# Squares, gating, value products and row transposes moved to other engines and steps in a hybrid retention and attention layer

## The chip, the cores and the metric

The kernel runs on one core of one Trainium2 chip. The metric is the device time of one execution in microseconds; the median of several runs counts. A core has TensorE (PE, with its weight loads PEld), VectorE (DVE), ScalarE (ACT), GpSimd (POOL) and SyncE (SP), which issues nearly all transfers of this kernel. Each engine works through its own instructions in the order in which the program gives them.

## The reference

One layer of a diffusion transformer over 2048 rows of width 1024, with 256 rows of context. It has a bidirectional retention (4 heads, in chunks of 128 rows), a grouped-query attention (8 query heads, 2 key heads, 64 wide, over context and rows) and a squared-relu MLP:

```python
h = _modulate(_rmsnorm(x, norm1_g), sh1, sc1)
rq, rk, rv, rg, aq, ak, av = jnp.split(h @ w_in, SPLIT_IDX, axis=-1)
...
ret, _, _ = _bidir_retention(rq_h, rk_h, _heads(rv, RET_HEADS), log_gamma, s_f, s_b)
ret = _ret_out(ret, rg, ret_gn_g)
...
att = _latent_attention(q, k, v, kc, vc)
x = x + g1 * (jnp.concatenate([ret, att], axis=-1) @ w_out)
h2 = _modulate(_rmsnorm(x, norm2_g), sh2, sc2)
x = x + g2 * (jnp.square(jax.nn.relu(h2 @ w_ff1)) @ w_ff2)
...
return _rmsnorm(x, final_norm_g)
```

## The kernel before

All products keep nearly full precision: each operand is split into a high and a low half, and three matmuls (high by high, high by low, low by high) stand for one. The order of work is written out by hand. Each part of the program enters its functions in a table by step and phase, and a loop runs the steps one after another and the phases of a step in a fixed order. So the order on every engine is the order of this table, and an engine runs ahead of the others only as far as waits and buffers let it.

**Projections** (to about 650 us). `do(s, part, fn)` enters a function; a step `s` is the product of one tile of 128 rows with one block of 512 columns of w_in (L1063 to L1065). The parts of a step run in the order hi, evac, turned, low, vec, pool, root, aux, turn, load, store. Beside the products run the tables of decay for the retention (`decay_tables`: a logarithm as a series on VectorE, `power` on VectorE, exponentials on ScalarE), the first 12 forward states of the retention (`forward_state`: load k and v of a chunk, weigh k by the decay on GpSimd at L1027, four products on TensorE at L1032, update on VectorE, store; one state in three steps), and the values' halves (`value_parts`). The tile `early` holds the tables' working space first and then k, v and the state. Keys are turned on TensorE (L744) and copied from PSUM by VectorE (L749). The low halves of the weights are made on VectorE (L516).

**Attention** (about 650 to 1650 us). Steps are entered with `on(k, phase, fn)`; the phases run in this order:

```python
PHASES = ("begin", "scores", "piece", "maximum", "early", "exp", "cast", "low", "chain", "pe", "values")
PHASES += ("late", "dma")
```

32 groups (16 tiles of rows by 2 key heads) of 18 steps each follow one another. In a step, TensorE makes one tile of scores (L209, L210) of one group and one piece (L172) for the row maxima of the next group; VectorE reduces the piece (L185), ScalarE takes the exponential (L215) into `p32` (three buffers of two steps each). Every two steps ScalarE casts a pair of tiles to fp16 (`phi`, L219), the low half `plo` is made on GpSimd (L226, five pairs of nine) or on VectorE (L228, in two parts), and TensorE multiplies both halves with the values (L242, L243).

Among these steps lie the retention (`retention(k0)`: five forward and two backward states at steps from `k0`, then one chunk in every RF = 35 steps), the gated halves of w_out (`output_weights`) and the output product of one tile of rows in every 35 steps (`output_tile`). That function turns the retention's and the attention's rows (L1588), multiplies, adds the input on VectorE (L1610), scales the new rows on GpSimd (`norm`, L1630), transposes them (`transpose_x`, L1635), applies the modulation on VectorE (L1640) and adds the shift on GpSimd (L1645). All transposes use PSUM bank 1, as the retention's heads do. For four of the tiles, `h_pair` then forms sums of rows for the MLP. `more_keys` fills the additional key rows `ks2` of a group.

**Up phase** (about 1650 to 2210 us) and **down phase** (to the end). The MLP is done with seven products in place of eight (Strassen's scheme): for every block of 256 of the 4096 columns, seven sums of quarters of w_ff1 are made on GpSimd and split on ScalarE (L1813) and VectorE (L1819). `up_part` multiplies them with seven sums of the rows; `up_out` combines the results on VectorE (L1849). For every finished quarter, relu on ScalarE (L1853) and a square on GpSimd (L1854) follow, and a store two steps on. In the same steps `seven` prepares w_ff2: it loads two blocks of rows, multiplies them by the gate (`gated`, L1892), makes sums on GpSimd (L1896) and splits on ScalarE (L1901) and VectorE (L1907). The phases of a step here are:

```python
FPHASES = ("pe", "sum", "hi", "lo", "relu", "out", "square", "late", "dma")
```

Of the kernel before, what the change touches and what calls it, by code (L numbers as in the profile page):

```python
# [13 lines left out]
F16 = mybir.dt.float16  # L14
BF16 = mybir.dt.bfloat16
I32 = mybir.dt.int32
AF = mybir.ActivationFunctionType
# [39 lines left out]
def layer_kernel(ctx: ExitStack, tc: tile.TileContext, a: dict, out: bass.AP):  # L57
# [89 lines left out]
    class Group:  # L147
# [69 lines left out]
        def cast(self, j):  # L217
            hi = self.hi[j] = pp.tile([P, 2, 512], F16, name="phi", tag="phi")
            nc.scalar.activation(hi, self.p[j], AF.Copy)  # L219

        def low(self, j, i=None):
            if i in (None, 0):
                self.lo[j] = pp.tile([P, 2, 512], F16, name="plo", tag="plo")
            lo, p, hi = self.lo[j], self.p[j], self.hi[j]
            if i is None:
                nc.gpsimd.tensor_tensor(lo, p, hi, op=ALU.subtract)  # L226
            else:
                nc.vector.tensor_tensor(lo[:, i], p[:, i], hi[:, i], op=ALU.subtract)  # L228
# [38 lines left out]
    with ExitStack() as st, tc.manual_schedule():  # L267
# [671 lines left out]
        def decay_tables(s):  # L939
# [14 lines left out]

            def series():
                u, w1, z, zz, lg = (x[v] for v in ("u", "w1", "z", "zz", "lg"))
                nc.vector.tensor_scalar(w1, u, -1.0, 1.0, op0=ALU.mult, op1=ALU.add)
                nc.vector.tensor_scalar(z, u, -1.0, 2.0, op0=ALU.mult, op1=ALU.add)
                nc.vector.reciprocal(z, z)
                nc.vector.tensor_mul(z, z, u)  # L960
                nc.vector.tensor_mul(zz, z, z)
                nc.vector.tensor_scalar(lg, zz, 1.0 / 17, 1.0 / 15, op0=ALU.mult, op1=ALU.add)
                for k in range(13, 0, -2):
                    nc.vector.tensor_mul(lg, lg, zz)
                    nc.vector.tensor_scalar_add(lg, lg, 1.0 / k)
                nc.vector.tensor_mul(lg, lg, z)
                nc.vector.tensor_scalar_mul(lg, lg, -2.0)

# [36 lines left out]
            do(s + 2, "hi", base)  # L1005
            do(s + 3, "aux", series)
            do(s + 4, "hi", log)
            do(s + 5, "aux", choose)
            for h in range(4):
                do(s + 6, "aux", power, h)  # L1010
                do(s + 7, "hi", tables, h)
            do(s + 7, "hi", rest)
            do(s + 8, "aux", diagonal)

        states = {}

        def forward_state(s, c):

            k, v = (early[:, 512 * i : 512 * i + 512].rearrange("p (h d) -> p h d", h=4) for i in range(2))
            st = early[:, 1536:2048].rearrange("p (h d) -> p h d", h=4)  # L1020

            def load():
                for to, src in ((k, rk_d[c]), (v, rv_d[c])):
                    nc.sync.dma_start(to.rearrange("p h d -> p (h d)"), src)

# [20 lines left out]

            do(s, "load", load)
            do(s + 1, "pool", weigh)
            do(s + 2, "turn", product)
            do(s + 3, "vec", update)  # L1050
            if c > 0:
                do(s + 4, "store", keep_state)

# [293 lines left out]
    def attention():  # L1347
        for n, g in enumerate(groups):
# [28 lines left out]
        return NK * len(groups) + LAG + 8  # L1377

# [198 lines left out]
    def output_tile(t, k, last):  # L1577
# [263 lines left out]
    def up_out(at, n, i, hf):  # L1841
# [10 lines left out]
        def done(r, f, tg):  # L1852
            on(at + 1, "relu", lambda: nc.scalar.activation(r, r, AF.Relu, scale=scu))  # L1853
            on(at + 2, "square", lambda: nc.gpsimd.tensor_tensor(r, r, r, op=ALU.mult))  # L1854
            on(at + 4, "dma", store_u, ITEMS[n][0], hf, 2 * tg + f, r)
# [23 lines left out]
    def seven(b0, source, tiles, low, kinds, scale=None, gate=None):  # L1879
# [10 lines left out]
        def gated(g):  # L1890
            w, eng = x["raw", g], nc.vector if g else nc.gpsimd
            eng.tensor_tensor(w, w, ff["g2"], op=ALU.mult)  # L1892

# [356 lines left out]
```

## Time and profile before

| | |
|---|---|
| median of three runs | 2811.19 us (2808.23 to 2811.27) |
| profiled execution | 2814.1 us |
| its span, first to last instruction | 2812.3 us |
| TensorE busy | 2673.6 us (95%) |
| VectorE busy | 2122.4 us (75%) |
| GpSimd busy | 1886.5 us (67%) |
| ScalarE busy | 1463.5 us (52%) |
| mean granted clock of TensorE | 0.990 |

A line such as `PE o L242 <- POOL plo L226: 17.9, 15, 2.5` (the whole span) reads: TensorE, before an instruction of line 242 that writes `o`, stood idle until an instruction of GpSimd at line 226 that writes `plo` was done; 17.9 us in all, in 15 waits, the longest 2.5 us. In a row of stretches, the span of the stretch comes first, then the busy time of each engine with the number of its instructions, then the granted clock of TensorE as a share of full speed, the transfers' share and GB/s. In a row of a group of instructions, busy time in us and the mean of one in ns follow the count, and then the idle time of the engine just before them and what ended it. In a row in order of time, the start and the length in us come first.

### The profile page before, as it was taken

Reading aid. Unit: us, or ns where it says so; the run is one execution under the profiler, and the core shown is the slowest. Engines: PE = TensorE matmul, PEld = TensorE weight load, DVE = VectorE, ACT = ScalarE, POOL = GpSimd, SP = SyncE. Lnnn points to the kernel's source line nnn. Section 1 sums busy time; section 2 is a strip of 40 time slices with the busy share of each in tenths; the row PEclk is TensorE's granted clock in tenths of the full one; section 3 lists DMA queues with packets and bytes.
Section 4 is the critical chain, followed back from the end, with each engine's and each line's share of the span. In section 5 each row is a group of like instructions: output and inputs, shape, how many; then the busy total and the mean of one; then the engine's idle time right before and its main releaser. Section 6 shows DMA issues by size and latency. Waiting matters only on the chain. (4 is left out here: it accounts for less than half of the span.)

```text
span 2812.3 us, 45879 instructions
## 1 busy us (share of the span) xinstructions
PE 2673.6 (95%) x16756; PEld 1605.7 (57%) x16756; DVE 2122.4 (75%) x3061; ACT 1463.5 (52%) x2442; POOL 1886.5 (67%) x1453
## 2 busy tenths in 40 slices
PE   6999999997799999999999999999999999999998
PEld 3878788875566666556666644444444444444444
DVE  3678847777987787777877568999999766556686
ACT  2534443325777777777777745544555422222243
POOL 2537427535766667886666679988888766666686
PEclk9999999999999999999999999999999999999999
DMA  6776876856211214332121174666777757575543
GB/s 214 262 263 195 289 277 205 288 190 189 66 52 52 66 59 119 96 99 85 63 91 45 64 255 143 191 211 201 230 251 239 260 183 277 177 261 196 180 159 126
DMA packets 329775, 482.86 MB, mean 172 GB/s; under 512 B 81990, under 2 KB 192838, under 8 KB 325068
## 3 DMA queue, kind: packets, MB, share of 16 engines
q1 hardware_dynamic: 329164, 479.66, 51.6%
q8 instruction: 132, 2.16, 0.3%
q14 instruction: 95, 0.78, 0.1%
q10 hardware_dynamic: 384, 0.26, 0.0%
HBM read 327.64 MB, written 152.19 MB: 171 GB/s over the span
## 5 line engine op out<-in xcount | busy, mean ns | idle before, releaser
L185 DVE TENSOR_REDUCE nm<-mp 128x1 f32<-128x512 f32 (+1 forms) x576 | 390.1, 684 | 171.0 <-PE mp L172 145.6
L226 POOL TENSOR_TENSOR plo<-p,phi 128x1024 f16<-128x1024 f32 x160 | 355.1, 2220 | 171.4 <-ACT phi L219 141.3
L215 ACT ACTIVATE p<-st 128x512 f32<-128x512 f32 x576 | 338.7, 597 | 197.7 <-PE st L210 127.5
L1839 PE MATMUL pu<-hf,w1f 128*128 128x512 f16 x896 | 339.7, 379 | 4.6 <-DVE w1f L1819 4.4
L1837 PE MATMUL pu<-hf,w1f 128*128 128x512 f16 x896 | 339.6, 379 | 1.8 <-DVE r L1849 1.8
L2063 PE MATMUL pd<-w,uf 128*128 128x512 f16 x896 | 339.6, 379 | 0.0
L2064 PE MATMUL pd<-w,uf 128*128 128x512 f16 x896 | 339.6, 379 | 0.0
L2065 PE MATMUL pd<-w,uf 128*128 128x512 f16 x896 | 339.6, 379 | 0.0
L1838 PE MATMUL pu<-hf,w1f 128*128 128x512 f16 x896 | 339.6, 379 | 0.0
L219 ACT ACTIVATE phi<-p 128x1024 f16<-128x1024 f32 x288 | 303.9, 1055 | 0.0
L2083 POOL TENSOR_TENSOR y<-y,d 128x512 f32<-128x512 f32 x128 | 210.5, 1646 | 137.8 <-ACT uf L2052 90.8
L1065 PE MATMUL pso<-whi,hlo_l 128*128 128x512 f32 (+1 forms) x768 | 290.1, 378 | 10.6 <-DVE hlo_l L492 10.5
L1063 PE MATMUL pso<-whi,hhi_l 128*128 128x512 f32 (+1 forms) x768 | 299.1, 389 | 0.0
L1064 PE MATMUL pso<-wlo,hhi_l 128*128 128x512 f32 (+1 forms) x768 | 288.0, 375 | 0.6 <-DVE wlo L516 0.6
L242 PE MATMUL o<-wv,plo 128*128 128x65 f16 x2304 | 234.8, 193 | 25.0 <-POOL plo L226 17.9
L228 DVE TENSOR_TENSOR plo<-p,phi 128x512 f16<-128x512 f32 x256 | 239.1, 934 | 19.5 <-ACT phi L219 14.2
L242 PEld LDWEIGHTS <-plo 128*128 128x128 f16 x2304 | 206.3, 98 | 69.3 <-POOL plo L226 26.0
L243 PE MATMUL o<-wv,phi 128*128 128x129 f16 x2304 | 242.6, 220 | 0.0
L209 PE MATMUL st<-qr,ks 128*128 128x512 f16 x576 | 220.3, 383 | 8.0 <-ACT p L215 7.6
L172 PE MATMUL mp<-ks,qr 128*128 128x512 f16 x512 | 197.2, 385 | 26.2 <-DVE nm L185 25.9
L210 PE MATMUL st<-qr,ks 128*128 128x512 f16 x576 | 220.7, 383 | 0.4
L243 PEld LDWEIGHTS <-phi 128*128 128x128 f16 x2304 | 205.4, 97 | 20.7
(331 smaller groups left out, 6093.4 us busy)
## 6 DMA issues: line engine op xcount, KB each, us to landing
wm<-in_w_ff SPq DMA_DIRECT2D x64, 512.0 KB, 7.1
u<-r SPq DMA_DIRECT2D x128, 256.0 KB, 4.0
ur<-u SPq DMA_DIRECT2D x128, 256.0 KB, 6.4
y<-x SPq DMA_DIRECT2D x64, 512.0 KB, 7.2
wst<-in_w_in SPq DMA_DIRECT2D x60, 512.0 KB, 6.7
wf<-w2f SPq DMA_DIRECT2D x112, 256.0 KB, 3.6
w<-wf SPq DMA_DIRECT2D x28, 1024.0 KB, 10.8
w1r<-in_w_ff SPq DMA_DIRECT2D x48, 512.0 KB, 5.1
```

Source lines behind the costliest of these rows:

```text
L185: nc.vector.tensor_reduce(dst, src, axis=AX.X, op=ALU.max, negate=True)
L215: nc.scalar.activation(self.p[kt // 2][:, kt % 2], self.s.pop(kt), AF.Exp, scale=HD**-0.5)
L219: nc.scalar.activation(hi, self.p[j], AF.Copy)
L226: nc.gpsimd.tensor_tensor(lo, p, hi, op=ALU.subtract)
L242: mm(o[:, : HD + 1], lo[:, i, c], v[:, : HD + 1], start=False, stop=False)
L243: mm(o, hi[:, i, c], v[:, :VW], start=False, stop=last)
L1837: mm(pu[hf, i], whi, hi, start=k == 0, stop=False)
L1838: mm(pu[hf, i], whi, lo, start=False, stop=False)
L1839: mm(pu[hf, i], wlo, hi, start=False, stop=k == 3)
L2063: mm(ps, u[:, 0, b], w[:, b, 0], start=b == 0, stop=False)
L2064: mm(ps, u[:, 0, b], w[:, b, 1], start=False, stop=False)
L2065: mm(ps, u[:, 1, b], w[:, b, 0], start=False, stop=b == 3)
```

## The change

Up phase: the square runs on ScalarE, in the step after its relu, instead of on GpSimd in that step, and both gating passes run on GpSimd; before, the second was on VectorE. Attention: the products with the values come one step later, with four buffers each instead of three for `phi` and `plo`; the end of a group moves by one step with them, and the loop is one step longer. The transposes of the new rows come at steps 39 and 41 of a tile instead of 27 and 28 (but for the last but one tile, which keeps 31 and 32), and all that follows on them moves along. The retention's first steps begin four steps later, the second group's extra keys 4, 3 and 2 steps later. Projections: the products of the states stand two steps behind the weighing instead of one, with k loaded one step ahead and k and v rotating through three places of `early`; the decay tables begin one step later, with the series on three steps and the powers on two; the value parts begin two steps later.

```diff
         def cast(self, j):
-            hi = self.hi[j] = pp.tile([P, 2, 512], F16, name="phi", tag="phi")
+            hi = self.hi[j] = pp.tile([P, 2, 512], F16, name="phi", tag="phi", bufs=4)
...
-                self.lo[j] = pp.tile([P, 2, 512], F16, name="plo", tag="plo")
+                self.lo[j] = pp.tile([P, 2, 512], F16, name="plo", tag="plo", bufs=4)
...
-            def series():
+            def series(i):
...
-                for k in range(13, 0, -2):
+                for k in ((13, 11), (9, 7, 5), (3, 1))[i]:
...
-            do(s + 3, "aux", series)
-            do(s + 4, "hi", log)
-            do(s + 5, "aux", choose)
+            for i in range(3):
+                do(s + 3 + i, "aux", series, i)
+            do(s + 5, "hi", log)
+            do(s + 6, "aux", choose)
             for h in range(4):
-                do(s + 6, "aux", power, h)
-                do(s + 7, "hi", tables, h)
-            do(s + 7, "hi", rest)
-            do(s + 8, "aux", diagonal)
+                do(s + 7 + h // 2, "aux", power, h)
+                do(s + 8 + h // 2, "hi", tables, h)
+            do(s + 8, "hi", rest)
+            do(s + 10, "aux", diagonal)
...
-            k, v = (early[:, 512 * i : 512 * i + 512].rearrange("p (h d) -> p h d", h=4) for i in range(2))
-            st = early[:, 1536:2048].rearrange("p (h d) -> p h d", h=4)
+            k, v, st = (
+                early[:, 512 * i : 512 * i + 512].rearrange("p (h d) -> p h d", h=4)
+                for i in (2 * c % 3, (2 * c + 1) % 3, 3)
+            )
...
-            do(s, "load", load)
+            do(s - 1 if c else s, "load", load, k, rk_d[c])
+            do(s, "load", load, v, rv_d[c])
             do(s + 1, "pool", weigh)
-            do(s + 2, "turn", product)
-            do(s + 3, "vec", update)
+            do(s + 3, "turn", product)
+            do(s + 4, "vec", update)
             if c > 0:
-                do(s + 4, "store", keep_state)
+                do(s + 5, "store", keep_state)
...
-        value_parts(first[2, C_RK] + 4)
-        decay_tables(first[1, C_AKV] + 4)
+        value_parts(first[2, C_RK] + 6)
+        decay_tables(first[1, C_AKV] + 5)
...
-                on(k + 2 * j + 6, "values", g.values, j)
-            k += NK + 5
+                on(k + 2 * j + 7, "values", g.values, j)
+            k += NK + 6
...
-        return NK * len(groups) + LAG + 8
+        return NK * len(groups) + LAG + 9
...
-            at = k + (31 if t == 1 else 27) + q
+            at = k + (31 + q if t == 1 else 39 + 2 * q)
             on(at, "pe", transpose_x, q)
...
-        on(26 + 4 * i, "late", more_keys, 1, i)
+        on(30 + 3 * i, "late", more_keys, 1, i)
     done = attention()
-    retention(24)
+    retention(28)
...
             on(at + 1, "relu", lambda: nc.scalar.activation(r, r, AF.Relu, scale=scu))
-            on(at + 2, "square", lambda: nc.gpsimd.tensor_tensor(r, r, r, op=ALU.mult))
+            on(at + 2, "relu", lambda: nc.scalar.activation(r, r, AF.Square))
             on(at + 4, "dma", store_u, ITEMS[n][0], hf, 2 * tg + f, r)
...
         def gated(g):
-            w, eng = x["raw", g], nc.vector if g else nc.gpsimd
-            eng.tensor_tensor(w, w, ff["g2"], op=ALU.mult)
+            w = x["raw", g]
+            nc.gpsimd.tensor_tensor(w, w, ff["g2"], op=ALU.mult)
...
-                on(b0 - 2 + g, "lo" if g else "sum", gated, g)
+                on(b0 - 2 + g, "sum", gated, g)
```

More of the change, by code (lines that the diff above doesn't have):

```diff
@@ L953, in base @@
                 nc.scalar.activation(x["u"], x["lr"], AF.Exp)
-            def series():
+            def series(i):
                 u, w1, z, zz, lg = (x[v] for v in ("u", "w1", "z", "zz", "lg"))
[L957 to L962, printed above, removed]
-                for k in range(13, 0, -2):
+                if i == 0:
+                    nc.vector.tensor_scalar(w1, u, -1.0, 1.0, op0=ALU.mult, op1=ALU.add)
+                    nc.vector.tensor_scalar(z, u, -1.0, 2.0, op0=ALU.mult, op1=ALU.add)
+                    nc.vector.reciprocal(z, z)
+                    nc.vector.tensor_mul(z, z, u)
+                    nc.vector.tensor_mul(zz, z, z)
+                    nc.vector.tensor_scalar(lg, zz, 1.0 / 17, 1.0 / 15, op0=ALU.mult, op1=ALU.add)
+                for k in ((13, 11), (9, 7, 5), (3, 1))[i]:
                     nc.vector.tensor_mul(lg, lg, zz)
                     nc.vector.tensor_scalar_add(lg, lg, 1.0 / k)
-                nc.vector.tensor_mul(lg, lg, z)
-                nc.vector.tensor_scalar_mul(lg, lg, -2.0)
+                if i == 2:
+                    nc.vector.tensor_mul(lg, lg, z)
+                    nc.vector.tensor_scalar_mul(lg, lg, -2.0)
             def log():
@@ L1005, in decay_tables, with load @@
             do(s + 2, "hi", base)
-            do(s + 3, "aux", series)
-            do(s + 4, "hi", log)
-            do(s + 5, "aux", choose)
+            for i in range(3):
+                do(s + 3 + i, "aux", series, i)
+            do(s + 5, "hi", log)
+            do(s + 6, "aux", choose)
             for h in range(4):
-                do(s + 6, "aux", power, h)
-                do(s + 7, "hi", tables, h)
-            do(s + 7, "hi", rest)
-            do(s + 8, "aux", diagonal)
+                do(s + 7 + h // 2, "aux", power, h)
+                do(s + 8 + h // 2, "hi", tables, h)
+            do(s + 8, "hi", rest)
+            do(s + 10, "aux", diagonal)
         states = {}
         def forward_state(s, c):
-            k, v = (early[:, 512 * i : 512 * i + 512].rearrange("p (h d) -> p h d", h=4) for i in range(2))
-            st = early[:, 1536:2048].rearrange("p (h d) -> p h d", h=4)
-            def load():
-                for to, src in ((k, rk_d[c]), (v, rv_d[c])):
-                    nc.sync.dma_start(to.rearrange("p h d -> p (h d)"), src)
+            k, v, st = (
+                early[:, 512 * i : 512 * i + 512].rearrange("p (h d) -> p h d", h=4)
+                for i in (2 * c % 3, (2 * c + 1) % 3, 3)
+            )
+            def load(to, src):
+                nc.sync.dma_start(to.rearrange("p h d -> p (h d)"), src)
             def weigh():
```

## The prediction

> **What bounds the kernel now.** I read first the busy time by stage, cut where the work changes: start, projections, filling of the attention pipeline, attention, drain, up phase, down phase.
>
> ```profile
> core 0: us, PE busy (x) PEld busy (x) DVE busy (x) ACT busy (x) POOL busy (x), PEclk, DMA share, GB/s
> 0.00:100.00 100.00, 73.44 (x425) 49.32 (x426) 46.33 (x102) 33.28 (x66) 31.96 (x56) 0.98 0.63 206
> 100.00:650.00 550.00, 536.27 (x2676) 441.02 (x2675) 403.74 (x658) 227.43 (x402) 257.44 (x280) 0.99 0.72 244
> 650.00:760.00 110.00, 81.08 (x725) 53.56 (x724) 97.19 (x152) 74.99 (x121) 78.43 (x51) 0.94 0.47 141
> 760.00:1612.00 852.00, 802.27 (x7453) 527.31 (x7453) 652.79 (x1136) 646.75 (x1058) 585.02 (x436) 0.99 0.25 73
> 1612.00:1650.00 38.00, 32.84 (x182) 16.46 (x180) 17.16 (x24) 11.88 (x24) 19.47 (x19) 0.96 0.83 320
> 1650.00:2210.00 560.00, 552.77 (x2553) 248.62 (x2551) 524.89 (x521) 289.40 (x455) 503.37 (x326) 1.00 0.65 205
> 2210.00:2812.30 602.30, 594.89 (x2757) 269.46 (x2754) 380.29 (x473) 179.81 (x323) 410.82 (x290) 1.00 0.58 205
> ```
>
> TensorE is the bound almost everywhere: it idles 13.7 us in the projections (550 less 536.27), 28.9 in the filling, 49.7 in the attention, 7.2 in the up phase. The change removes no matmul. So it can gain only what stands in these gaps, plus what they cost in clock, and it loses only where it opens new ones. The second view, TensorE's waits in each stage (us in total, times, longest), says who opens them. In order: two lines from 100 to 650 us, three from 650 to 760, five from 760 to 1610, three from 1650 to 2210.
>
> ```profile
> PE psx L744 <- DVE ks L749: 6.2, 2, 5.8
> PE psf L1032 <- POOL early L1027: 2.8, 1, 2.8
> ```
> ```profile
> PE mp L172 <- DVE nm L185: 15.0, 14, 2.1
> PE st L209 <- ACT p L215: 6.0, 2, 4.7
> PE o L242 <- DVE plo L228: 3.1, 4, 1.2
> ```
> ```profile
> PE o L242 <- POOL plo L226: 17.6, 14, 2.5
> PE mp L172 <- DVE nm L185: 11.0, 20, 2.2
> PE bank L1635 <- POOL xr L1630: 7.2, 8, 2.4
> PE bank L1588 <- DVE u L1640: 3.9, 10, 0.8
> PE o L242 <- DVE plo L228: 3.7, 6, 1.8
> ```
> ```profile
> PE pu L1839 <- DVE w1f L1819: 4.4, 8, 1.4
> PE pu L1837 <- DVE r L1849: 1.8, 2, 1.6
> PE bank L1635 <- DVE u L1640: 0.8, 1, 0.8
> ```
>
> Nearly each of these rows is met by one part of the diff. What is left to find is how much of each wait goes and how much comes back elsewhere.
>
> **Projections: decay tables and states.** The 5.8 us wait at about 285 us is VectorE's queue:
>
> ```profile
> 278.05 0.28 DVE L982 TENSOR_SCALAR early<-early 128x128 f32<-128x128 f32 x1
> ...
> 281.67 3.49 DVE L516 TENSOR_TENSOR wlo<-wst,whi 128x1024 fp32r<-128x1024 f32 x3
> 285.07 0.42 DVE L749 CAST ks<-psx 128x256 f16<-128x256 f32 x1
> ```
>
> The eight instructions of `power` fill 278.05 to 281.67, then three weight halves take 3.49 us, and only then comes the copy that frees TensorE's bank. The tables now begin one step later, the series takes three steps, and `power` falls two and three steps later than before, behind these weight halves. So 3.6 us leave the queue ahead of the copy, and 2.2 of the 5.8 remain (bounds 0 and 5.8, since the series now runs closer to the copy). Gain 3.6. The state product now stands two steps behind GpSimd's weighing, so its 2.8 us wait goes whole. In return the load of v(c) waits for the product of state c-1 in the same step, and the weight fetches queued behind it on SyncE wait too; those are issued up to five steps ahead of use, which hides it. If that cover is gone, the cost is about one wait of the size of the one removed, 2.8 us. The value parts start two steps later and still end before the projections do: 0.
>
> **The clock.** Gaps cost more than their idle time:
>
> ```profile
> 250.00:300.00 50.00, 44.21 (x197) 35.23 (x196) 45.48 (x96) 27.15 (x57) 31.91 (x38) 0.93 0.85 286
> ```
> ```profile
> 1285.00:1290.00 5.00, 3.19 (x22) 2.38 (x23) 2.03 (x3) 1.47 (x2) 5.00 (x4) 0.55 0.26 52
> ```
>
> The first row lost 0.07 x 50 = 3.5 us of clock around the 5.8 us wait; I take 2 of it. The second fell to 0.55 among the attention's waits on GpSimd, the longest of which is 2.4 us: 0.45 x 5 = 2.3 us lost there. The whole attention stage, at 0.99, lost some 0.01 x 852 = 8.5. I take 3 (bounds 0 and 8.5). The Trainium skill (TensorE: Matmul & The Clock Gate, What's actually happening) says that the clock halves only after an idle window of about 3.4 us and returns after a busy one. By that rule alone waits of 2.5 us would cost no clock and the 3 would be 0, with a sum of 41 in place of 44; the 0.55 row speaks for the larger figure. Projections together: 3.6 + 2.8 + 2 = 8.4.
>
> **Filling, 650 to 760 us.** One wait on exp lasts 4.7 us:
>
> ```profile
> 664.91 1.26 POOL L1555 TENSOR_TENSOR wos<-wos,g1b 128x512 f32<-128x512 f32 x1 [3.03 <-DMA wos<-in_w_out]
> ```
>
> GpSimd gates the first rows of w_out at 664.91, after waiting for their transfer; ScalarE's copy of them stands in front of an exp, and TensorE waits for that exp. `retention(28)` puts its first loads four steps later, so that the gates and w_out are no longer behind them on SyncE, and the extra key rows of the second group come 4, 3 and 2 steps later. Of the 6.0 us I take 4 (bounds 0 and 6.0). I take nothing of the 15.0 behind L185 nor of the 3.1 behind L228: VectorE is 97.19 of 110 us busy here, so its throughput decides.
>
> **Attention: values one step later.** A step is
>
> ```profile
> L242 PE MATMUL o<-wv,plo x2304: 191/193/262, 671.6 to 1614.3; 128*128 128x65 f16 x192
> ```
>
> 942.7 us for 288 pairs of steps, 1.64 us a step. All 14 waits on GpSimd's low halves together are 17.6 us, 1.26 each, the longest 2.5; VectorE's six are 3.7. With one more step ahead of `values` a wait of mean size is covered, and the longest leaves 2.5 - 1.64 = 0.9. The two tags get the fourth buffer that the longer life needs; the probabilities (p32) keep three. That limits the gain, for ScalarE's exp waits on the same low halves through p32:
>
> ```profile
> ACT p L215 <- POOL plo L226: 26.9, 18, 3.8
> ```
>
> A late half now meets the next scores rather than the values; I leave 4 us for that. Gain 21.3 - 4 = 17 (bounds 5 and 21). TensorE then asks sooner for the maxima's banks, and VectorE is 77% busy (652.79 of 852): the 11.0 us behind L185 grow, and I charge 3 (bounds 0 and 10).
>
> **Attention: transposes of the new rows 12 to 13 steps later.** They used to come three steps after the scaling on GpSimd (L1630) was issued, and shared bank 1 with the next tile's transposes (L1588). At 39 and 41 they lie behind that tile's use of the bank, two steps apart, and the scaling has 15 steps. 7.2 + 3.9 = 11.1 us of waits go; I take 10, as the product for the next head may now wait once for the same bank. The addition of shifts (two per tile) moves away from the stretch in which GpSimd does decays, scaling and weighing. The stores and the pairing of half the rows move with them, and SyncE passes the next gate load a little later; that load is used eight steps on, so nothing waits. x lives 43 steps instead of 30 with tiles 35 apart and four buffers: no wait. Attention together: 17 - 3 + 10 + 3 = 27.
>
> **Up phase.** The prices are in these rows:
>
> ```profile
> L1854 POOL TENSOR_TENSOR r<-r 128x512 f32<-128x512 f32 x128 | 181.0, 1415 | 29.5 <-ACT r L1853 29.3
> ...
> L1853 ACT ACTIVATE r<-r,scu 128x512 f32<-128x512 f32 x128 | 91.9, 718 | 143.9 <-DVE r L1849 143.2
> ...
> L1892 POOL TENSOR_TENSOR b<-b,g2b 128x1024 f32<-128x1024 f32 x16 | 42.2, 2636 | 0.4 <-DMA b<-in_w_ff 0.4
> ...
> L1892 DVE TENSOR_TENSOR b<-b,g2b 128x1024 f32<-128x1024 f32 x16 | 33.1, 2071 | 0.5 <-DMA b<-in_w_ff 0.5
> ```
>
> GpSimd loses 181.0 us of squares and takes 16 x 2.636 = 42 us of gating: 503 - 139 = 364 of 560 us. VectorE loses 33.1: 525 to 492, the only engine that TensorE waits for here (4.4 + 1.8). ScalarE gains 128 squares; by the relu's 0.718 us that is 92 us, 289 to 381 of 560. It waits 143 us for VectorE's sums already, so its queue has room. If that room were gone, a w1 half late on ScalarE would reach TensorE through L1819. Gain 6 of the 6.2 (bounds 0 and 7.2, the stage's whole gap). The square is issued one step behind its relu, as before, so the stores keep their slot. Down phase: no change. The loop over the attention is one step longer; at its end TensorE waits on the chain of the last tile, so I charge 1 (bounds 0 and 1.64).
>
> **Sum.** 8.4 + 4 + 27 + 6 - 1 = 44 us. The profiled execution took 2814.1 us for a span of 2812.3, so it becomes 2770; against the median of 2811.2 the same 44 gives **2767**. Its own range, from the bounds above taken two thirds of the way, is 2748 to 2786.
>
> **Rivals.** *Buffers give back the gain* (0.16): the late low halves hold p32, exp waits, scores wait. For it: the 26.9 us above. Against it: scores of the next step come after nearly a whole step of other matmuls. Then values gain 5 instead of 17 and L185 takes 10 instead of 3, gain 25: 2786, at most 2797. *The postponing only postpones* (0.09): the waits of the attention come from GpSimd's backlog (5.00 of 5 us in the row at 1285), and a backlog meets any phase. Against it: GpSimd is 585 of 852 us busy over the stage. What is left is 8.4 + 4 + 6 - 1 = 17, or half that if the startup transfer is late anyway: 2794 to 2803, and 0.04 of these 0.09 for a result that can't be told from no change.
>
> *Slower* (0.05): Square and Relu lie in different function sets of ScalarE, so each of 128 pairs loads a table twice.
>
> ```profile
> L1617 ACT ACTIVATE junk<-xr 128x512 f32<-128x512 f32 x32 | 20.1, 629 | 21.3 <-DVE xr L1610 20.9
> ...
> L215 ACT ACT_TABLE_LOAD x1 | 1.3, 1283 | 0.0
> ```
>
> 256 x 1.283 = 328 us against 560 - 381 = 179 us of room: 150 us too many, 2767 + 150 = 2917. It decides from (179 + 44) / 1.283 = 174 loads. Against it: L1617 is a Square amid the exps of L215, and L215 shows one load in all. The Trainium skill (ScalarE: Activation LUTs, Table sets: the hidden batching unit) names relu, copy, identity and abs as present in every set, and square not among them; strictly read it allows this rival, and the trace, with its one load, leaves it small.
>
> **How the numbers follow.** The forecast has 0.70. The range 2747 to 2797 holds it and the first rival. A measurement of this kernel tells about 0.2% (5.6 us) from no change. Faster 0.70 + 0.16 + 0.05 = 0.91, same 0.04, slower 0.05.
>
> **What would show it.** Right: L242's waits under 6 us and L1635's and L1588's near zero in the attention; L744 at 2 to 3 us; L1032 gone; no TensorE wait in the up phase, with GpSimd near 364 us and ScalarE near 381; L185 up by a few us; one table load at L215. Wrong: new waits of L209 on exp over 10 us, L185 over 20 us from 760 on, GpSimd's halves still over 10 us, or table loads in the up phase.

## The result and the profile after

The changed kernel takes 2797.5 us (median of six runs, 2796.4 to 2802.3) against 2811.2 beside it (2807.9 to 2814.5). The ratio is 0.9955, with a 95% interval of [0.9943, 0.9968]: faster by 14 us, not by 44. A few executions of 3116 us or more are left out of the medians and ratios below. In the changed kernel's lines, everything below the diff's insertions is renumbered: L744 and L749 stay, L1032 is L1036, L1588 is L1593, L1635 is L1640, L1839 is L1844, L1849 is L1854.

First starts of a line show in which part the time changed. The rows are TensorE's first score and its first product of the up phase, of the kernel before and then of the kernel after (durations of one in ns, then the first and the last start in us):

```profile
L209 PE MATMUL st<-qr,ks x576: 376/379/634, 653.5 to 1609.7; 128*128 128x512 f16 x192
L1837 PE MATMUL pu<-hf,w1f x896: 376/379/379, 1633.0 to 2223.9; 128*128 128x512 f16 x180
```
```profile
L209 PE MATMUL st<-qr,ks x576: 376/379/634, 659.6 to 1599.8; 128*128 128x512 f16 x192
L1842 PE MATMUL pu<-hf,w1f x896: 379/379/379, 1624.8 to 2206.8; 128*128 128x512 f16 x180
```

The projections lost 6.1 us (653.5 to 659.6). From the first score to the up phase 979.5 became 965.2, a gain of 14.3. The up phase went from 590.9 to 582.0, a gain of 8.9. The rest stayed at 588.4 (spans 2812.3 and 2795.2). The sum is 17.1 between these two executions. So the forecast failed in two places: a loss where 8.4 were expected, and about half of what filling, attention and end together (4 + 27 - 1 = 30) were to give.

The busy time by stage of the kernel after, cut at the places that moved:

```profile
core 0: us, PE busy (x) PEld busy (x) DVE busy (x) ACT busy (x) POOL busy (x), PEclk, DMA share, GB/s
100.00:656.00 556.00, 536.45 (x2652) 438.81 (x2651) 401.96 (x654) 226.27 (x398) 249.75 (x276) 0.99 0.71 239
656.00:770.00 114.00, 83.17 (x745) 56.31 (x744) 102.45 (x158) 78.19 (x125) 81.45 (x53) 0.93 0.45 136
770.00:1606.00 836.00, 794.25 (x7474) 525.17 (x7472) 657.29 (x1134) 635.54 (x1058) 579.44 (x435) 1.00 0.26 76
1640.00:2200.00 560.00, 558.57 (x2591) 253.31 (x2590) 464.89 (x511) 358.32 (x584) 365.56 (x221) 1.00 0.66 208
```

**Attention.** TensorE's waits from 770 to 1606 us, the kernel after, and ahead of them two rows of the kernel before in the same stretch, which were too small to be argued from:

```profile
PE mp L196 <- DVE mt L191: 2.1, 3, 0.9
PE st L209 <- ACT p L215: 1.6, 5, 0.6
```
```profile
PE mp L172 <- DVE nm L185: 14.2, 21, 2.2
PE o L242 <- POOL plo L226: 8.0, 5, 3.6
PE st L209 <- ACT p L215: 7.1, 18, 1.1
PE mp L196 <- DVE mt L191: 6.7, 7, 1.7
PE bank L1593 <- POOL ma L261: 1.8, 1, 1.8
PE mp L176 <- DVE nm L185: 1.7, 4, 0.8
```

The rows that the change was argued from did shrink. L242 behind GpSimd fell from 17.6 to 8.0, its waits on VectorE are gone, and L1635 and L1588 lost their 7.2 and 3.9. But the rest of the list grew: L209 by 5.5, L196 by 4.6, L172 by 3.2, L176 and the bank behind L261 by 3.2. TensorE reached the next stop earlier and stood there. Over 770 to 1605 us its idle time fell by only 6.8 (47.9 to 41.1). The clock that was not granted, summed over the 167 stretches of 5 us, fell by 4.4 (6.8 to 2.4). From the first score to the up phase, where both executions do the same work (8266 and 8269 matmuls in the traces), idle time fell by 6.9 and the clock not granted by 3.4. The other 4.0 of the 14.3 us lie in the busy time of the matmuls and are not explained.

**Up phase.** One wait is left, that of the last rows' transposes; behind it the rows of the moved work, then the row of VectorE's halves of w_ff2, before (L1907) and after (L1912), from 1640 to 2200 us:

```profile
PE bank L1640 <- DVE u L1645: 1.4, 1, 1.4
```
```profile
L1897 POOL TENSOR_TENSOR b<-b,g2b 128x1024 f32<-128x1024 f32 x32 | 82.7, 2590 | 18.9 <-DMA b<-in_w_ff 18.9
L1859 ACT ACTIVATE r<-r 128x512 f32<-128x512 f32 x124 | 76.2, 615 | 0.3
```
```profile
L1907 DVE SCALAR_TENSOR_TENSOR w2f<-b,scw,w2f 128x512 f16<-128x512 f32 x64 | 97.5, 1529 | 0.0
```
```profile
L1912 DVE SCALAR_TENSOR_TENSOR w2f<-b,scw,w2f 128x512 f16<-128x512 f32 x64 | 82.0, 1287 | 0.0
```

**Projections.** The stop at L744 did not go, and a new one stands at 320 to 335 us, where the kernel before ran without a gap. TensorE's waits from 100 to 656 us, the stretches around the new stop, VectorE's queue ahead of the key copy, and the new stop on ScalarE, VectorE and TensorE, all of the kernel after:

```profile
PE psx L744 <- DVE ks L749: 6.0, 2, 4.4
PE pso L1069 <- DVE wlo L516: 5.6, 4, 3.2
```
```profile
320.00:325.00 5.00, 3.32 (x15) 2.43 (x13) 0.82 (x2) 1.45 (x3) 1.04 (x1) 1.00 1.06 405
325.00:330.00 5.00, 2.27 (x11) 1.63 (x11) 4.89 (x7) 4.13 (x9) 2.22 (x2) 1.00 0.60 202
330.00:335.00 5.00, 3.87 (x10) 3.08 (x11) 5.00 (x6) 0.55 (x2) 0.92 (x1) 0.66 0.97 315
```
```profile
277.34 0.71 DVE L968 TENSOR_TENSOR early<-early 128x8 f32<-128x8 f32 x1
278.08 0.17 DVE L969 TENSOR_SCALAR early<-early 128x8 f32<-128x8 f32 x1
278.17 4.57 DVE L516 TENSOR_TENSOR wlo<-wst,whi 128x1024 fp32r<-128x1024 f32 x3
282.66 0.41 DVE L749 CAST ks<-psx 128x256 f16<-128x256 f32 x1
```
```profile
323.55 0.60 ACT L689 ACTIVATE qhl<-psx 128x512 f16<-128x512 f32 x1 [10.95 <-DMA aq<-qhl]
324.18 0.69 DVE L692 TENSOR_TENSOR qhl<-psx,qhl 128x512 f16<-128x512 f32 x1 [4.61 <-ACT qhl L689]
325.62 0.63 PE L618 MATMUL psx<-ident,ys 128*128 128x128 f32 x4 [2.29 <-DVE ys L559]
331.13 0.74 PE L1069 MATMUL pso<-wlo,hhi_l 128*128 128x512 f32 x1 [3.25 <-DVE wlo L516]
```

The line of L749 shows the copy in the same place as before: behind three weight halves, which now take 4.57 us in place of 3.49, with the series' last piece ahead of them instead of the powers. The last four lines are one chain. ScalarE must wait 10.95 us until a store of the turned queries has left its buffer; VectorE waits 4.61 us for ScalarE, and TensorE then twice for VectorE, whose later work has piled up behind that. Before, ScalarE's wait was

```profile
318.95 0.60 ACT L689 ACTIVATE qhl<-psx 128x512 f16<-128x512 f32 x1 [5.78 <-DMA aq<-qhl]
```

### The profile page after: what moved, and what is told of

Its sections match the earlier page's. It is cut to its first block, busy times and chain, and to the rows that moved or that the text cites. A ratio compares the mean times of both kernels' runs of the same rounds, so it can differ in the third digit from the quotient of the medians.

```text
span 2795.2 us, 45749 instructions
## 1 busy us (share of the span) xinstructions
PE 2663.1 (95%) x16756; PEld 1604.3 (57%) x16756; DVE 2067.6 (74%) x3045; ACT 1521.2 (54%) x2570; POOL 1730.2 (62%) x1341
## 4 chain that ended last, share of the span: by engine, by line
PE 62%; DVE 6%; POOL 3%; ACT 2%; issue 1%; DMA 1%; POOLq 0%; DVEq 0%; SPq 0%; ACTq 0%
PE pd L2068 7%; PE pd L2070 7%; PE pd L2069 7%; PE pu L1844 7%; PE pu L1842 7%; PE pu L1843 7%; PE o L243 3%; PE st L209 3%; PE st L210 3%; PE mp L172 3%; DVE plo L228 2%; DVE nm L185 2%; PE bank L1609 2%; PE bank L1610 2%; PE bank L1608 2%; PE o L242 2%
## 5 line engine op out<-in xcount | busy, mean ns | idle before, releaser
L185 DVE TENSOR_REDUCE nm<-mp 128x1 f32<-128x512 f32 (+1 forms) x576 | 389.9, 684 | 158.3 <-PE mp L172 134.8
L1844 PE MATMUL pu<-hf,w1f 128*128 128x512 f16 x896 | 339.6, 379 | 0.0
L242 PE MATMUL o<-wv,plo 128*128 128x65 f16 x2304 | 234.3, 193 | 8.0 <-POOL plo L226 8.0
L209 PE MATMUL st<-qr,ks 128*128 128x512 f16 x576 | 220.0, 382 | 19.2 <-ACT p L215 18.2
L242 PEld LDWEIGHTS <-plo 128*128 128x128 f16 x2304 | 208.1, 98 | 38.2 <-POOL plo L226 10.1
L172 PE MATMUL mp<-ks,qr 128*128 128x512 f16 x512 | 195.5, 382 | 26.3 <-DVE nm L185 26.0
```

The costliest lines, as they stand in the source:

```text
L185: nc.vector.tensor_reduce(dst, src, axis=AX.X, op=ALU.max, negate=True)
L209: mm(ps, ks[:, self.g, k], q[:, 0], start=True, stop=False)
L242: mm(o[:, : HD + 1], lo[:, i, c], v[:, : HD + 1], start=False, stop=False)
L1844: mm(pu[hf, i], wlo, hi, start=False, stop=k == 3)
```

## The experiments

Each edit is given against the kernel named; times are medians, and the ratio is to the kernel before on the same chip. "First score" and "attention" are the starts and distances read as above.

**The change less one part.** First the decay tables, then the states, are put back as they were before.

```diff
-                for k in ((13, 11), (9, 7, 5), (3, 1))[i]:
+                for k in range(13, 0, -2):
...
-                do(s + 7 + h // 2, "aux", power, h)
+                do(s + 6, "aux", power, h)
...
-        decay_tables(first[1, C_AKV] + 5)
+        decay_tables(first[1, C_AKV] + 4)
```

> The changed kernel with the decay tables as before (one step earlier, the series in one piece, the powers on one step); all else changed. Theory: the new place of the tables is what makes the projections 6 us longer, by VectorE's and ScalarE's queues around 280 and 320 us. Then the first scores (L209) begin at 650 to 652 us instead of 659.6, the waits of TensorE from 320 to 335 us (8 us in the changed kernel) go, and the time is 2788 to 2792. Rival, the states' loads on SyncE do it: the first scores stay at 658 to 660 and the time at 2797.

2790.5 us, 0.9917 [0.9899, 0.9935], first score at 654.2, and TensorE is busy throughout 320 to 335 us (15.00 of 15). The decay tables' new place and their spread together cost 5.4 us by the first score and 7.0 by the medians.

```diff
-            do(s - 1 if c else s, "load", load, k, rk_d[c])
-            do(s, "load", load, v, rv_d[c])
+            do(s, "load", load)
...
-            do(s + 3, "turn", product)
+            do(s + 2, "turn", product)
```

> The changed kernel with the forward states as before (product one step behind the weighing, both loads in one step, two places); all else changed. Theory: the wait of 2.8 us on L1027's weighing comes back, nothing else moves: 2798 to 2801. Rival, SyncE's longer wait for the product (69.8 us instead of 50.5) delays the stores behind it and so makes the stop at 320 to 335 us: it goes, and the time falls to 2789 to 2792.

2793.6 us, 0.9929 [0.9914, 0.9944], first score still at 659.1. The loss isn't the states'. TensorE's wait behind the weighing is back (4.4 us, the longest 2.8), and the time is 3.9 us lower all the same, so no run shows that the new order of the states gained anything.

**One part alone, in the kernel before.** The up phase:

```diff
-            on(at + 2, "square", lambda: nc.gpsimd.tensor_tensor(r, r, r, op=ALU.mult))
+            on(at + 2, "relu", lambda: nc.scalar.activation(r, r, AF.Square))
...
-            w, eng = x["raw", g], nc.vector if g else nc.gpsimd
-            eng.tensor_tensor(w, w, ff["g2"], op=ALU.mult)
+            w = x["raw", g]
+            nc.gpsimd.tensor_tensor(w, w, ff["g2"], op=ALU.mult)
...
-                on(b0 - 2 + g, "lo" if g else "sum", gated, g)
+                on(b0 - 2 + g, "sum", gated, g)
```

> The kernel before with the edits of the up phase alone (squares on ScalarE, both gating passes on GpSimd). Theory: the parts add up, and this one takes the up phase's whole gap: from the first to the last matmul of the up phase 582.5 us instead of 591.3, time 2801 to 2804. Rival, the gain came from the earlier parts' new timing of transfers: under 3 us of gain, 2808 or more.

2802.9 us, 0.9965 [0.9952, 0.9978]. The up phase takes 581.1 us, and no wait of TensorE is left in it from 1640 to 2200. That is 10 us on its own; added to two other parts below it gives 7 by the medians (8.6 in the length of the phase).

The values one step later, with the fourth buffers and the ends of group and loop as in the change, of which one line is shown:

```diff
-                on(k + 2 * j + 6, "values", g.values, j)
+                on(k + 2 * j + 7, "values", g.values, j)
```

> The kernel before with values one step later and the fourth buffers alone. Theory: TensorE's waits on low halves (24.9 us) fall to 8, but some 10 us come back as waits of scores on exp and on the row maxima's products; gain 5 to 10 us, 2801 to 2806. Rival, the step is worth the 17 us that were forecast and the later transposes or the filling gave them back: 2792 to 2796. Other rival, backlog only: under 3 us of gain.

2811.7 us, 0.9997 [0.9988, 1.0007]: nothing by the times. In the trace the attention is 5 us shorter (974.5; the kernel before and the runs of the up phase alone and of the filling alone have 979.5, 978.1 and 978.6). Four of TensorE's waits from 770 to 1606 us of this kernel:

```profile
PE bank L1635 <- POOL xr L1630: 12.9, 8, 3.8
PE st L209 <- ACT p L215: 7.5, 17, 1.6
PE bank L1588 <- DVE u L1640: 5.2, 9, 1.4
PE o L242 <- POOL plo L226: 3.2, 1, 3.2
```

L242 has lost 14.4 of its 17.6 us, more than in the whole change. L1635, behind GpSimd's scaling of the new rows, grew by 5.7, L209 by 5.9, L1588 by 1.3. The transposes alone:

```diff
-            at = k + (31 if t == 1 else 27) + q
+            at = k + (31 + q if t == 1 else 39 + 2 * q)
```

> The kernel before with the new rows' transposes at 39 and 41 alone. Theory: the 11.1 us of waits at L1635 and L1588 go and little comes back, since they hang on GpSimd's backlog at one place and not on a buffer that others share: gain 6 to 10 us, 2801 to 2805. Rival, the backlog moves to the low halves, as with the values alone (no gain there): L242's waits rise above 30 us and the time stays at 2809 to 2813.

2816.9 us, 1.0019 [1.001, 1.0029]: slower, with 983.8 us of attention. L1635 and L1588 are gone from the list, and

```profile
PE o L242 <- POOL plo L226: 30.8, 20, 5.1
```

is what they turned into: GpSimd is as late as before, and TensorE now meets it at the low halves only. The filling:

```diff
-        on(26 + 4 * i, "late", more_keys, 1, i)
+        on(30 + 3 * i, "late", more_keys, 1, i)
...
-    retention(24)
+    retention(28)
```

> The kernel before with the retention's start four steps later and the second group's extra keys later, alone. Forecast of the record: 4 us of gain, 2807 to 2808. Rival: w_out's first rows still come late, since SyncE reaches their load only when the last stores of the projections are done; the wait on exp at the start stays over 3 us and the time within 2809 to 2813.

2812.7 us, 1.0001 [0.9991, 1.001]. The long wait on exp between 656 and 770 us lasts 4.5 us, against 4.7, although GpSimd begins to gate w_out 5.7 us after the first score here and 11.4 us after it before.

**Buffers.** A fourth buffer for the probabilities, and three of each high and low half, in the kernel after:

```diff
-                self.p[kt // 2] = pp.tile([P, 2, 512], F32, name="p32", tag="p32")
+                self.p[kt // 2] = pp.tile([P, 2, 512], F32, name="p32", tag="p32", bufs=4)
...
-            hi = self.hi[j] = pp.tile([P, 2, 512], F16, name="phi", tag="phi", bufs=4)
+            hi = self.hi[j] = pp.tile([P, 2, 512], F16, name="phi", tag="phi")
...
-                self.lo[j] = pp.tile([P, 2, 512], F16, name="plo", tag="plo", bufs=4)
+                self.lo[j] = pp.tile([P, 2, 512], F16, name="plo", tag="plo")
```

> The changed kernel with four buffers for p32 and three each for phi and plo. Theory: exp waits for the low halves through the three buffers of p32, and so gives back the values' gain; with four, L209's waits on exp fall from 18.2 to under 8 us and the time to 2789 to 2793. Rival: ScalarE, VectorE and GpSimd are late by their load, and one more buffer only moves the wait to L242, L172 or L196: 2796 to 2800.

2796.6 us, 0.9944 [0.9929, 0.9959]. Exp's waits from 770 to 1606 us for scores and low halves, kernel after and then this one:

```profile
ACT p L215 <- PE st L210: 131.5, 134, 2.8
ACT p L215 <- DVE plo L228: 22.0, 11, 4.6
ACT p L215 <- POOL plo L226: 20.5, 16, 3.7
```
```profile
ACT p L215 <- PE st L210: 171.3, 158, 5.6
ACT p L215 <- POOL plo L226: 2.3, 2, 1.1
```

Some 40 us of waiting for low halves became 40 us of waiting for scores, and the time stayed. TensorE's own waits moved as well: L209 fell by 4.5 us (to 2.6), and L172, L196 and L242 grew by 5.8 together. Then the last two edits of this diff without the first:

> The changed kernel with phi and plo at three buffers as before, p32 at three. It tells what part of the run with four for p32 comes from phi and plo. By the order of steps a cast of pair j+3 comes two steps after the values of pair j, so three buffers suffice: 2796 to 2799. Rival: the fourth buffers are needed, and casts wait for values: over 2801.

2801.2 us, 0.9951 [0.9933, 0.9969]: no difference from the kernel after (0.9955) can be told by the times, which scatter from 2793.8 to 2806.5. In its trace the attention takes 969.9 us (965.2 in the kernel after), so the fourth buffers of the halves may still be worth a few us.

**Parts together.** The diffs of the values and of the transposes shown above, in the kernel before:

> The kernel before with values one step later and the new rows' transposes later, together; nothing else. Theory: GpSimd's backlog has two consumers on TensorE, the values (through plo) and the transposes (through the scaled rows); with slack for one alone TensorE stops at the other (gains 1 and -5 us measured), with slack for both it runs on. From the first scores to the first matmul of the up phase 963 to 968 us (979.5 before), time 2797 to 2801. Rival, the parts add: 2814 to 2818. Other rival, the filling or the states gave the rest: 2805 to 2810.

2799.8 us, 0.9958 [0.9943, 0.9974]: -11 together, where apart they gave -1 and +5. The attention takes 963.3 us (before 979.5, with the values alone 974.5, with the transposes alone 983.8). With the diff of the up phase added:

> The kernel before with values, transposes and the up phase's edits; projections and filling as before. Theory: 9 to 10 us of the up phase come on top of the 13 of the pair, and the 6 to 7 us that the decay tables cost stay away: 2786 to 2791. Rival, the parts don't add across phases: 2794 or more.

2792.8 us, 0.9939 [0.9921, 0.9956]. With that of the filling too:

> As the run of values, transposes and up phase, with the retention's start and the second group's extra keys later as well. Theory: the filling is bound by VectorE (about 100 of 115 us busy) and by w_out's first rows, and neither changes: within 2 us of that run. Rival, it is of use once the values are late: 3 to 6 us less.

2791.3 us, 0.9929 [0.9913, 0.9945], with the old projections: all of the change but the decay tables and the states. It is the base of the runs below, but for the next, which stands on the one before.

**GpSimd's share of the low halves.** Six pairs of nine, then four, in place of five:

```diff
-POOL_PAIRS = (0, 2, 4, 6, 7)
+POOL_PAIRS = (0, 2, 3, 5, 6, 8)
```

> As the run of values, transposes and up phase, with six of nine low halves of a group on GpSimd instead of five (0, 2, 3, 5, 6, 8). It takes 32 x 2 x 0.95 = 61 us from VectorE in the attention and gives GpSimd 32 x 2.2 = 70. If what remains is VectorE's load (waits at L172, L176, L196, some 40 us of the changed kernel), the time falls by 4 to 10 us against that run. If it is GpSimd's backlog, waits at L242 and L209 rise above 40 us and the time rises by 5 to 20.

2802.6 us, 0.9978 [0.9968, 0.9988]: some 10 us worse than 2792.8.

```diff
-POOL_PAIRS = (0, 2, 4, 6, 7)
+POOL_PAIRS = (0, 2, 4, 6)
```

> The same parts with the old projections and four pairs of nine on GpSimd in place of five: GpSimd loses 32 low halves of 2.2 us, some 70 us, VectorE takes 61 us. Theory GpSimd: its load holds the remaining waits, so L242's waits on GpSimd go, 5 to 10 us less, 2781 to 2787. Theory balance: six pairs cost 11 us and four cost as much, because VectorE then makes the maxima late; L172's waits double to 50 us or more, 2798 to 2805.

2800.6 us, 0.9968 [0.9955, 0.9981]: 9 us worse than 2791.3. The largest row from 770 to 1606 us is, of six pairs and then of four:

```profile
PE o L242 <- POOL plo L226: 19.2, 11, 3.5
```
```profile
PE mp L172 <- DVE nm L185: 21.0, 27, 2.2
```

With five pairs the two rows are 7.9 and 14.2. A pair moved between the engines costs about 10 us either way (the attention grows by 14.6 and by 7.5). Six pairs also take other places in the group than the five did, and no other places were tried.

**The decay tables, spread or late.** The series on three steps and the powers on two from the old start:

```diff
-                for k in range(13, 0, -2):
+                for k in ((13, 11), (9, 7, 5), (3, 1))[i]:
...
-                do(s + 6, "aux", power, h)
+                do(s + 7 + h // 2, "aux", power, h)
```

> The values, transposes, up phase and filling of the change with the old projections, in which alone the series goes over three steps and the powers over two, from the old start. Theory spread: the pieces stand between other work of VectorE and delay SyncE's row of issues for longer, so the projections lose the 6 to 7 us here too: first score at 659 to 661 us, 2796 to 2799. Theory later start: the place does it and not the spread, first score at 652 to 654, 2789 to 2792.

2794.2 us, 0.9941 [0.9926, 0.9956], first score at 656.7. Both whole, one step later:

```diff
-        decay_tables(first[1, C_AKV] + 4)
+        decay_tables(first[1, C_AKV] + 5)
```

> The values, transposes, up phase and filling of the change with the old projections, in which the decay tables alone begin one step later and stay whole. Theory later start: the exponentials of the tables and the transfers behind them meet the turning of the query heads at 320 to 333 us, first score at 658 to 661, 2796 to 2799. Theory spread: nothing is lost, 652 to 654, 2789 to 2792.

2790.8 us, 0.9927 [0.991, 0.9944], first score at 654.0. From 320 to 335 us TensorE is busy 12.25 and 12.78 us of 15, against 15.00 in the base and 9.46 in the kernel after: each opens part of the stop. ScalarE's wait for its store is 10.68 and 9.94 us in them and 6.13 in the base, so either edit alone makes it long. In the kernels with the old tables the first score came at 650.8 to 656.3 us (13 traces), in those with the new ones at 659.1 to 663.3 (four). The late start alone falls into the first span and the spread alone just above it. Neither shows the whole loss alone, and with one trace each against a scatter of 5.5 us, how the two share it stays open.

**The scaling of the new rows on ScalarE.** Taken from GpSimd and not given to VectorE, in the base:

```diff
-            nc.gpsimd.tensor_scalar(y["x"], y["x"], y["r"], 1.0, op0=ALU.mult, op1=ALU.mult)
+            nc.scalar.activation(y["x"], y["x"], AF.Copy, scale=y["r"])
```

> The same parts with the old projections and the scaling of the new rows (32 instructions or fewer, 1.27 us each on GpSimd) on ScalarE. Theory GpSimd: 20 us less load in its densest stretch, 2 to 5 us less, 2786 to 2789. Theory ScalarE: the scaling stands among the exponentials, L209's waits on exp grow by as much as the scaling takes, 5 us or more, 2795 to 2800. Theory neutral: 2790 to 2792.

2783.4 us, 0.9907 [0.9891, 0.9922]: the fastest kernel of the study, 14 us below the change and 8 below its base. Three of TensorE's waits from 770 to 1606 us, and what moved:

```profile
PE st L209 <- ACT p L215: 20.3, 24, 3.0
PE mp L172 <- DVE nm L185: 10.6, 20, 1.4
PE bank L1588 <- DVE rl L1595: 4.0, 1, 4.0
```
```profile
L1630 ACT ACTIVATE xr<-xr,cy_f 128x1024 f32<-128x1024 f32 x16 | 18.4, 1153 | 14.0 <-DMA x<-xr 11.2 <-POOL cy_f L1339 2.8
```

No wait of L242 is left. L209 pays for it (6.9 to 20.3): ScalarE now holds the exponentials up while it waits for the rows' store to leave them. The attention takes 960.9 us (base 966.2, and 962.6 in the run before the filling was added), and the up phase, which the edit doesn't touch, 580.4 (base 584.3). The intervals of this run and its base overlap, so how much of the 8 us is the edit's own isn't shown. The same diff alone in the kernel before:

> The kernel before, in which only the scaling of the new rows stands on ScalarE: 16 instructions of 1.27 us less on GpSimd in the attention. Theory backlog: GpSimd's delay reaches TensorE through the low halves and through the scaled rows, and both waits fall with nothing postponed, L242 behind GpSimd from 17.9 to under 12 and L1635 gone, 2798 to 2804. Theory order: only the scaled rows come sooner, the low halves stay late, L242 stays at 17 or over and the exponentials wait for the scaling, 2808 to 2814.

2810.9 us, 0.9998 [0.9987, 1.0008]: nothing, where a plain backlog would have let both waits fall. Only its time is used, so where the freed time went isn't shown. With the diff of the transposes beside it:

> The kernel before with the transposes at 39 and 41 and the scaling of the new rows on ScalarE. The transposes alone moved the stop to the low halves, L242 behind GpSimd 31.1 us, 2817. Theory backlog: with 1.27 us less in each tile's dense stretch L242 falls to 15 to 20 and the run is at 2800 to 2808. Theory order: TensorE simply reaches the low halves sooner, L242 stays near 30, 2813 to 2818.

2798.7 us, 0.9951 [0.9933, 0.9968]: 18 us better than the transposes alone (attention 965.0 against 983.8), where the scaling alone was worth nothing.

```profile
PE o L242 <- POOL plo L226: 8.2, 11, 1.7
```

The 30.8 us that the transposes had left at the low halves fell to 8.2.

## Why the prediction was wrong

**Which stage binds** was right: TensorE bounds the kernel, and most of what was gained came from its gaps and their clock. The direction was right and the size was not, by terms that failed in different ways.

**Projections, forecast +8.4, measured -6.1.** The step "so 3.6 us leave the queue ahead of the copy" failed. The powers left, but the series' third piece and three slower weight halves stood there instead, and 4.4 of the 5.8 remained, against a forecast 2.2. The larger error is a place that the working never looked at: where the moved powers and tables would land. Their new place (the powers at 294 to 305 us) borders on a stretch in which ScalarE already waited 5.78 us for a store; it waited 10.95 there, and TensorE stood still for 5.5 us between 320 and 335. Putting the tables back recovers it, putting the states back doesn't. Through which of the queues the tables lengthen that wait wasn't separated. The states' wait of 2.8 us went as forecast, but no time came of it that a run shows. The 2 us of clock didn't come: the clock not granted from 100 to 655 us is 6.8 against 7.3.

**Filling, forecast +4, measured 0.** "So that the gates and w_out are no longer behind them on SyncE" came true. In the kernel after, GpSimd begins the gating 5.6 us after the first score, and 11.4 us after it before; exp's fourth tile starts 7.5 us after the first score instead of 13.2. The step that failed is "Of the 6.0 us I take 4". TensorE comes to the same score, its sixth, sooner as well, and stands there for nearly as long. GpSimd's gating in the kernel after, and TensorE's long wait before and after:

```profile
665.17 1.26 POOL L1560 TENSOR_TENSOR wos<-wos,g1b 128x512 f32<-128x512 f32 x1 [23.62 <-DMA qr<-aq]
```
```profile
667.37 0.59 PE L209 MATMUL st<-qr,ks 128*128 128x512 f16 x1 [4.73 <-ACT p L215]
```
```profile
667.63 0.58 PE L209 MATMUL st<-qr,ks 128*128 128x512 f16 x1 [4.38 <-ACT p L215]
```

The lead is gone by exp's eighteenth tile, which starts 38.8 us after the first score before, 38.9 in the run of the filling alone and 38.3 in the kernel after. In that run VectorE is busy 29.1 of the 31.0 us that follow the long wait. The prediction had said of this stage that VectorE's throughput decides, and had used it for L185 only; that it also took this gain fits the traces, but no run tests it.

**Attention, forecast +27, measured 14 with filling and end.** The gross part was nearly right: the rows named (L242 twice, L1635, L1588) lost 22.5 us of 30.5 (17.6, 1.8 in this stretch, 7.2 and 3.9, down to 8.0). The step that failed is what was charged against it: "I leave 4 us" for exp and "3" for the maxima, 7 in all, where 16.5 came back, in L209, L196, L172, L176 and the bank. The 3 of clock was near (4.4), and larger than the 0 of the rule quoted from the Trainium skill (TensorE: Matmul & The Clock Gate, What's actually happening), although no wait of this stage before was longer than 2.5 us. A second error lies in the form of the sum: "values +17" and "transposes +10" were added as if they were independent. They are two places at which TensorE meets one late engine. Alone, either moves the meeting to the other place (-1 and +5 us in time, 5.0 shorter and 4.3 longer in the attention); together they give 11 (16.2 in the attention). The step "a wait of mean size is covered, and the longest leaves 0.9" treated lateness as a fixed number per wait; the longest left is 3.6.

**Up phase, forecast +6, measured 8.9 (10 alone).** The mechanism was right step by step: GpSimd 365.56 us busy for a forecast 364, no wait behind VectorE left, no table load (the last one stands at 657.2 us). ScalarE got 358 for 381, since a square takes 0.615 us and not the relu's 0.718. VectorE went to 465 and not 492: its halves of w_ff2 take 1287 ns in place of 1529, which the sum had no term for. The bound of 7.2 us, "the stage's whole gap", was none: idle time fell by 5.8 (7.2 to 1.4), and 3.1 more came out of the busy time of as many matmuls (583.7 to 580.6). A matmul is booked here with 379 ns while they follow one another every 215 (580.6 us for 2694), so by an estimate from these rows the first 164 ns of every stall are not counted as idle; for the 11 waits of before that is 1.8 us.

**The rivals.** "Buffers give back the gain" is refuted for the 19 us that it charged: with a fourth buffer the wait it rests on goes and the time stays, within the scatter. "The postponing only postpones" named the right mechanism, a backlog that meets any phase, and holds for each postponement by itself; as a forecast of the sum it failed, as the two together do gain and the projections lose. Its objection, that GpSimd is busy 585 of 852 us only, proved no guide: from five pairs, one more or one fewer on GpSimd costs about 10 us. That no function table would be loaded between relu and square was right.

**The range.** "Its own range" doesn't follow from the bounds given. Two thirds of the way along them the gain runs from some 20 to 57 us, so from 2754 to 2791, and not from 2748 to 2786.

## What to carry to other kernels

Waits at several places for one late engine are one term, not several: postponing one consumer moves the wait to the next, and time came only from postponing both, or from postponing one and taking work off the late engine. A mean load of 70% doesn't rule such an engine out; move one unit of work each way and see whether both cost, and if so, look for a third engine with idle time, as ScalarE was here (with the transposes late, 2816.9 us became 2798.7). Before work is moved, read the queues where it will land with the same care as the place that it leaves, and ask what will bound the stage once the wait is gone.

## What the runs showed of the hardware that was not expected

VectorE's halves of w_ff2 (L1907, L1912 after) sped up by 16% (1529 to 1287 ns) when GpSimd's busy time in the stage fell from 503 to 366 us, though nothing about them was changed; with the up phase's edits alone they take 1269 ns. The halves of w_ff1 in the same stage, the same instruction, did not all follow (L1819: 1169 to 1197 and 1278 to 1164 ns). Whether GpSimd's load causes it wasn't tested. Clock was lost among short waits: where the transposes alone lengthened the waits at L242 to 30.8 us in 20 pieces, none over 5.1, the clock not granted from 770 to 1605 us rose from 6.8 to 12.0 us; in the changed kernel, with no wait there over 3.6, it was 2.4. It doesn't simply follow the idle time: with the scaling on ScalarE TensorE idles about as long in that stretch as in the changed kernel (42.2 and 41.1 us) and loses 8.6 us of clock.
